# Product-key experts on one core: first gates written straight into their tile, one-hots made for four tokens at a time, first query group projected list by list

## The chip, the cores and the metric

One core of one Trainium2 chip runs the whole program. The metric is device time in microseconds (us) of one execution. Engines are named as in the profile: PE is TensorE (PEld its weight loads), DVE VectorE, ACT ScalarE, POOL GpSimd, SP SyncE, which issues most DMAs.

## The reference, cut to what matters

The program computes two transformer blocks over 512 tokens of width 1024. The change lies in the last part of the second block, a layer of 128 x 128 experts that are addressed by product keys:

```python
q = (t @ w_query).reshape(n_tok, P_HEADS, 2, P_DQ)            # 8 heads, 2 halves, 128 wide
sc = jnp.einsum('thcd,hckd->thck', q, sub_keys)               # 16 lists of 128 scores per token
s1, i1 = lax.top_k(sc[:, :, 0], P_TOPK)                       # best 16 of each list
s2, i2 = lax.top_k(sc[:, :, 1], P_TOPK)
cand = (s1[..., :, None] + s2[..., None, :]).reshape(n_tok, P_HEADS, P_TOPK * P_TOPK)
top_s, top_i = lax.top_k(cand, P_TOPK)                        # best 16 pairs of each head
e1 = jnp.take_along_axis(i1, top_i // P_TOPK, axis=-1)
e2 = jnp.take_along_axis(i2, top_i % P_TOPK, axis=-1)
gates = jax.nn.softmax(top_s, axis=-1)
act = jax.nn.gelu(einsum('td,tkd->tk', tb, expert_u[eb])) * gb
return einsum('tk,tkd->td', act, expert_v[eb])
```

## The kernel before, in words

Everything below is in `peer` and its helpers. The 512 tokens are four blocks of 128. Three blocks are "dense": for them all 16384 experts are computed, in 128 pieces of 128 experts, and a dense matrix of gates, zero where an expert was not chosen, weights them. The fourth block is "sparse": its chosen rows are gathered by indirect DMA.

**Queries and lists.** `w_query` is 1024 x 2048, that is 16 lists (head and half) of 128 columns. `proj` handles a group of four lists: for each of 8 row tiles of the weights it loads 128x512, ACT casts the high part (w_hi, L291), POOL subtracts to get the low part (w_lo, L293), and PE does three matmuls for each of four column blocks, so a list of the group is finished only when all four are, after 96 matmuls (L308, `acc`). `pick` then multiplies each block's queries with the keys (L2026, `sc`), ACT copies the scores (`scs`, L2029), and DVE takes the best 16 of each list (`top16`: five instructions, L2313 to L2317). `peer_pairs` forms candidate pairs on POOL (`cand`, `pr_w`, `pr_st`, `p_oh`) and picks the best 16 pairs on DVE. Its steps are mixed with the next lists.

**First pieces.** Each of the 128 pieces has a first half: load 128x1024 of `expert_u` (`p_raw`), cast (`p_hi`, ACT), subtract (`p_lo`, L2218, POOL for the first 13 pieces, then DVE), 24 matmuls into `pu`, gelu. 36 first halves (LAG) run ahead of the second halves; 15 (LEAD) are issued before the gates begin.

**Gates.** `peer_gates` (L2221 on) builds the gate matrix of the 384 dense tokens. For each token there are two one-hots of 128x128: o1 marks the first index, o2 the second, scaled by the gate; their product on PE (`pg`, L2235) is the 128x128 gates of that token. Before, each one-hot is a `tensor_scalar` with the index (and gate) as per-partition scalars: o2 always on DVE (L2234), o1 on DVE or POOL (L2232), eight buffers each. Four tokens fill one PSUM tile; ACT copies it into `gst` (L2236). Every 16 tokens ACT's queue writes 1 MB to the DRAM tensor `gates_d`. There are 96 such groups of four tokens, mixed with first halves of pieces 15 on.

**Second halves.** `load_gates` (L2071) reads 8 pieces' gates (`gt`, 1.5 MB) from `gates_d` on SP's queue. DVE multiplies `act` with them (L2082), ACT and DVE split the product (`ahi`, `alo`), and PE accumulates `py`. From there PE alternates between `pu` of piece c and `py` of piece c - 36.

The order of each engine's instructions is fixed when the program is built, by a scheduler that hoists instructions of the written order; each engine then runs its own list in order and waits where it must.

Of the kernel before, what the change touches and what calls it, by code (L numbers as in the profile page):

```python
# [9 lines left out]
F32 = mybir.dt.float32  # L10
# [3 lines left out]
U32 = mybir.dt.uint32  # L14
AF = mybir.ActivationFunctionType
ALU = mybir.AluOpType
# [4 lines left out]
P = 128  # L21
D = 1024
S = 512
NB = S // P
# [154 lines left out]
class Net:  # L179
# [1023 lines left out]

        return self.mod_c[:, split * 8:split * 8 + 8, s]

    def proj2(self, c0, n, acts, evac, lo_eng=None):


        nc = self.nc
        w_ap = self.a["w_in_2"][0]  # L1210
        lo_eng = lo_eng or nc.vector
        nt = (n + P - 1) // P
        kt = min(KC, 512 // n)
        main, ctx = acts
        ps = [self.psa.tile([P, 512], F32, tag="acc", name="acc2") for _ in range(nt)]
        pc = self.psa.tile([P, 2, 256], F32, tag="acc", name="acc_c") if ctx is not None else None
        for kk in range(KC // kt):
            raw = self.ws.tile([P, 512], F32, tag="w_raw", name="w_raw", bufs=3)[:, :kt * n].rearrange("p (k c) -> p k c", k=kt)
            nc.sync.dma_start(out=raw, in_=w_ap[kk * kt * P:(kk + 1) * kt * P, c0:c0 + n].rearrange("(k p) c -> p k c", p=P))
            hi = self.ws.tile([P, 512], F32R, tag="w_hi", name="w_hi")[:, :kt * n].rearrange("p (k c) -> p k c", k=kt)  # L1220
            lo = self.ws.tile([P, 512], F32R, tag="w_lo", name="w_lo")[:, :kt * n].rearrange("p (k c) -> p k c", k=kt)
            nc.scalar.copy(hi, raw)  # L1222
            lo_eng.tensor_tensor(lo, raw, hi.bitcast(F32), op=ALU.subtract)  # L1223
            for k2 in range(kt):
                k = kk * kt + k2
                st, sp = k == 0, k == KC - 1
                for j in range(nt):
                    m = min(P, n - j * P)
                    js = slice(j * P, j * P + m)
                    w = (hi[:, k2, js], lo[:, k2, js])  # L1230
                    self.mm3(ps[j][:m], w, main[k], st, sp)
                    if ctx is not None:
                        self.mm3(pc[:m, j], w, ctx[k], st and j == 0, sp, shared=True)
        for j in range(nt):
            evac(j, ps[j], pc[:, j] if ctx is not None else None)
# [739 lines left out]
    def peer(self):  # L1975
# [3 lines left out]
        nc, a = self.nc, self.a  # L1979
        tt, ts, stt = nc.vector.tensor_tensor, nc.vector.tensor_scalar, nc.vector.scalar_tensor_tensor  # L1980
        dense, sparse = range(ND), range(ND, NB)
        order = [*sparse, *dense]
        T = ND * P
# [7 lines left out]
        with self.pool("px") as xp:  # L1991
# [12 lines left out]
            hT = self.hT2  # L2004
# [12 lines left out]
        with self.pool("pe", 2, side="right") as ep:  # L2017
            best = {b: [tp.tile([P, 8, 16], F32, name=f"{n}{b}", bufs=1) for n in ("top", "e0", "e1")] for b in range(NB)}
            keys = tp.tile([P, 16, P], F32, name="pkeys", bufs=1)
            nc.sync.dma_start(out=keys, in_=a["sub_keys_2"].rearrange("h c d k -> d (h c) k"))  # L2020

            def pick(g, qT):
                for b in order:
                    ps = self.pt("sc").rearrange("p (n k) -> p n k", n=4)
                    for n in range(4):
                        nc.tensor.matmul(ps[:, n, :], qT[n][:, b * P:(b + 1) * P], keys[:, g * 4 + n, :],  # L2026
                                         start=True, stop=True)
                    sc = tp.tile([P, 4, P], F32, tag="sc", name="scs")
                    nc.scalar.copy(sc, ps)  # L2029
                    v16 = tp.tile([P, 4, 16], F32, tag="v16", name="v16", bufs=3)  # L2030
                    i16 = tp.tile([P, 4, 16], U32, tag="i16", name="i16", bufs=3)
                    i16f = tp.tile([P, 4, 16], F32, tag="i16f", name="i16f", bufs=3)
                    for n in range(4):
                        self.top16(v16[:, n, :], i16[:, n, :], sc[:, n, :], tp)
                        pending[:] = [p for p in pending if next(p, True) is None]
                        yield
                    nc.vector.tensor_copy(i16f, i16)
                    pending.append(pairs(g, b, v16, i16f))
# [4 lines left out]
                    self.peer_choice(best[b], tp, idx.get(b), gate.get(b), eg.get(b))  # L2043
            steps, pending = iter(()), []
            self.pool_turns = (0, 1, 2, 3)
            for g in range(4):
                qT = []

                def ev(j, ps):
                    t = tp.tile([P, S], F32, tag=f"pq{j}", name=f"pq{j}")  # L2050
                    nc.scalar.copy(t, ps)
                    qT.append(t)
                self.proj(a["w_query_2"][0], g * 512, hT, True, ev, between=lambda: [next(steps, None) for _ in range(2)])
                for _ in steps:
                    pass
                steps = pick(g, qT)
            dots = {b: ep.tile([P, P], F32, name=f"dots{b}", bufs=1) for b in sparse}
            y = {b: ep.tile([P, D], F32, name=f"py{b}", bufs=1) for b in sparse}
            acts, ps, gt = [], {}, []

            def first(c):
                hi, lo = self.peer_piece(a["expert_u_2_T"][c], ep, nc.gpsimd if c < LEAD - 2 else nc.vector)
# [6 lines left out]
                acts.append(act)  # L2069

            def load_gates(c):  # L2071
                t = sp.tile([P, T // 16, 8, 16], F32, tag="gt", name="gt")
                nc.sync.dma_start(out=t, in_=G[:, :, c:c + 8, :].rearrange("g p e t -> p g e t"))
                gt.append(t)

# [45 lines left out]
            n = 16  # L2121
            for c in range(LAG):
                if c == LEAD:
                    for _ in itertools.chain(steps, (x for p in pending for x in p)):
                        pass
                    tst.close()
                    gst = ExitStack()
                    gp = gst.enter_context(self.pool("pgs", 2))
                    steps = (None for b in dense for _ in self.peer_gates(b, eg[b], iota, G, gp))
                    n = T // 4  # L2130
                left = max((LEAD if c < LEAD else LAG - 3) - c, 1)
                first(c)
                for _ in range(-(-n // left)):
                    next(steps, None)
                    n -= 1
# [14 lines left out]
                nc.scalar.activation(out=junk, in_=o[:, hf * 512:(hf + 1) * 512], func=AF.Square, accum_out=ss[:, hf, b:b + 1])  # L2150

            with self.pool("ps", 2) as sp, self.pool("pu", 1, side="right") as gu:
                load_gates(0)
                held = []
                ps.update({(b, hf): self.psa.tile([P, 512], F32, tag="acc", name="py") for b in dense for hf in range(2)})
                for c in range(LAG, P + LAG):
                    if c < P:
                        first(c)
                    held.append(second(c - LAG))
                    ins = held[-1][1]  # L2160
                    if c < P + LAG - 2:
                        products(*held.pop()[0])
                    with self.tc.issue_after(ins.ins):
                        while done < 2 * P * len(sparse) and done * spread < c + 1 - LAG + min(c + 1, P) - LAG:
                            next(rows)
                            done += 1
                for b in sparse:
                    o = y[b]
                    nc.sync.dma_start(out=hN[b], in_=xd[b * P:(b + 1) * P, :])
                    tt(o, o, g2, op=ALU.mult)  # L2170
                    nc.gpsimd.tensor_tensor(o, o, hN[b], op=ALU.add)
                    for hf in range(2):
                        finish_squares(o, hf, b)

                for part in ((dense[:-1],), (dense[-1:], (0,)), (dense[-1:], (1,))):
                    for (args, _) in held:
                        products(*args, *part)
            with self.pool("pf") as fp:
# [18 lines left out]
                for b in (*sparse, *reversed(dense)):  # L2197
# [2 lines left out]
                    stt(o[:, 512:], o[:, 512:], rb, fw[:, 512:], op0=ALU.mult, op1=ALU.mult)  # L2200
                    nc.sync.dma_start(out=dst[b * 16:(b + 1) * 16], in_=o)
            fst.close()
            self.php_st.close()

    def gather(self, rows, idx, gu):
# [12 lines left out]
        (eng or self.nc.vector).tensor_tensor(lo, raw, hi.bitcast(F32), op=ALU.subtract)  # L2218
        return hi, lo

    def peer_gates(self, b, eg, iota, G, ep):  # L2221


        nc = self.nc
        for t in range(0, P, 4):
            if t % 16 == 0:
                st = ep.tile([P, P, 16], F32, tag="gst", name="gst")
            pg = self.tr("pg").rearrange("p (t e) -> p t e", t=4)
            for q in range(4):
                e1, e2, g = (eg[:, n, t + q:t + q + 1] for n in range(3))  # L2230
                o1 = ep.tile([P, P], F32, tag="oh1", name="oh1", bufs=8)
                (nc.vector if q >= 2 + t // 4 % 2 else nc.gpsimd).tensor_scalar(o1, iota, e1, None, op0=ALU.is_equal)  # L2232
                o2 = ep.tile([P, P], F32, tag="oh2", name="oh2", bufs=8)
                nc.vector.tensor_scalar(o2, iota, e2, g, op0=ALU.is_equal, op1=ALU.mult)  # L2234
                nc.tensor.matmul(pg[:, q, :], o2, o1, start=True, stop=True)  # L2235
            nc.scalar.copy(st.rearrange("p e t -> p t e")[:, t % 16:t % 16 + 4, :], pg)  # L2236
            if t % 16 == 12:
                nc.scalar.dma_start(out=G[(b * P + t) // 16], in_=st)
            yield

    def peer_pairs(self, v16, i16f, best, tp):
# [152 lines left out]
```

## Time and profile before

| What | Value |
| --- | --- |
| Median of 3 runs | 4377.47 us (4374.94 to 4378.69) |
| The profiled execution, its time | 4381.8 us |
| Its span | 4379.9 us, 59166 instructions |
| Busy share of the span | PE 93%, DVE 63%, ACT 38%, POOL 26% |
| Granted TensorE clock, mean | 0.965 |
| Queries begin on PE | 3003 us from the span's start |
| First `sc` product | 3033.80 us |
| One-hots begin on DVE | 3227.14 us |
| Last `pg` product done, `pu` alone follows | 3404.65 us |
| First `py` | 3424.66 us |

Times inside the execution are counted from the start of the span. The span ends 1.9 us short of the execution's time. A busy share averages over the whole program; the rows further down are cut to the stretch from 3003 us to 3520 us, where the change lies.

### The profile page before, as it was taken

How to read it: one execution, taken by the hardware profiler on the slowest of the kernel's cores; microseconds unless marked ns; L12 is line 12 of the kernel's file. 1: busy time of each engine (PE TensorE's matmuls, PEld its weight loads, DVE VectorE, ACT ScalarE, POOL GpSimd, SP SyncE). 2: the span in 40 equal slices, each digit the busy share in tenths (PEclk: the TensorE clock that was granted, in tenths of full speed). 3: DMA queues.
4: the chain of work that ended last, by engine and by line, in shares of the span. 5: the costliest groups of instructions: out<-in, count | busy, mean ns of one | idle time of the engine just before them, and what ended most of it. 6: DMA issues, size and time to landing. Idle time of an engine off the chain costs nothing. (4 is left out here: it accounts for less than half of the span.)

```text
span 4379.9 us, 59166 instructions
## 1 busy us (share of the span) xinstructions
PE 4054.2 (93%) x21308; PEld 3139.6 (72%) x21309; DVE 2778.6 (63%) x6214; ACT 1683.9 (38%) x3192; POOL 1150.9 (26%) x1089
## 2 busy tenths in 40 slices
PE   8999899999988998898898898898889899999998
PEld 6677544666665446777786777676679789988886
DVE  5455455553644556777767655636999777777776
ACT  4544211544441134445544444323256333333333
POOL 2001100100021013222102212125679344444443
PEclk9999999999999998989899999899999999999999
DMA  4145697222458951222121112134145988888875
GB/s 135 31 119 151 256 418 323 80 87 76 113 190 336 420 219 48 54 57 54 48 61 50 50 49 56 58 113 130 58 152 198 310 303 298 305 292 305 289 267 196
DMA packets 342588, 739.73 MB, mean 169 GB/s; under 512 B 72512, under 2 KB 175024, under 8 KB 314640
## 3 DMA queue, kind: packets, MB, share of 16 engines
q1 hardware_dynamic: 277536, 540.54, 36.9%
q0 software_dynamic: 45376, 167.76, 10.4%
q10 hardware_dynamic: 19376, 27.57, 1.7%
q8 instruction: 171, 2.80, 0.3%
q14 instruction: 129, 1.06, 0.1%
HBM read 694.07 MB, written 41.70 MB: 168 GB/s over the span
## 5 line engine op out<-in xcount | busy, mean ns | idle before, releaser
L308 PE MATMUL acc<-rn_hi,w_lo 128*128 128x512 f32 x1224 | 506.1, 414 | 36.9 <-DVE w_lo L1223 13.1
L308 PE MATMUL acc<-rn_hi,w_hi 128*128 128x512 f32 x1224 | 506.9, 415 | 32.3 <-ACT w_hi L1222 16.9
L308 PE MATMUL acc<-rn_lo,w_hi 128*128 128x512 f32 x1224 | 500.7, 409 | 2.0 <-POOL rn_lo L275 2.0
L293 POOL TENSOR_TENSOR w_lo<-w_raw,w_hi 128x512 fp32r<-128x512 f32 x103 | 136.3, 1325 | 1041.1 <-ACT w_hi L291 839.8
L2217 ACT CAST p_hi<-p_raw 128x1024 fp32r<-128x1024 f32 x256 | 268.4, 1049 | 333.5 <-PE pu L308 241.7
L308 PE MATMUL pu<-rn_hi,p_lo 128*128 128x384 f32 x1024 | 350.8, 343 | 17.7 <-POOL p_lo L2218 14.9
L291 ACT CAST w_hi<-w_raw 128x512 fp32r<-128x512 f32 x316 | 195.8, 621 | 435.0 <-PE acc L308 325.3
L308 PE MATMUL pu<-rn_hi,p_hi 128*128 128x384 f32 x1024 | 348.8, 341 | 5.3 <-ACT p_hi L2217 4.2
L308 PE MATMUL pu<-rn_lo,p_hi 128*128 128x384 f32 x1024 | 348.5, 340 | 0.0
L2218 DVE TENSOR_TENSOR p_lo<-p_raw,p_hi 128x1024 fp32r<-128x1024 f32 x243 | 297.4, 1224 | 73.2 <-ACT p_hi L2217 73.2
L293 DVE TENSOR_TENSOR w_lo<-w_raw,w_hi 128x512 fp32r<-128x512 f32 x213 | 149.7, 703 | 268.6 <-ACT w_hi L291 257.2
L308 PE MATMUL py<-p_hi,ahi 128*128 128x512 f32 x768 | 305.5, 398 | 6.6 <-ACT ahi L274 5.2
L308 PEld LDWEIGHTS acc<-rn_hi,w_lo 128*128 128x128 f32 x1224 | 237.5, 194 | 102.6 <-POOL w_lo L293 19.2
L308 PE MATMUL py<-p_lo,ahi 128*128 128x512 f32 x768 | 305.0, 397 | 2.3 <-DVE p_lo L2218 2.3
L308 PE MATMUL py<-p_hi,alo 128*128 128x512 f32 x768 | 304.9, 397 | 0.0
L308 PEld LDWEIGHTS acc<-rn_hi,w_hi 128*128 128x128 f32 x1224 | 237.4, 194 | 75.9 <-ACT w_hi L1222 19.3
L308 PEld LDWEIGHTS acc<-rn_lo,w_hi 128*128 128x128 f32 x1224 | 237.9, 194 | 34.8 <-POOL rn_lo L275 3.2
L2207 POOL DMA_INDIRECT eu<-in_expert_v_dram,idx x128 | 189.1, 1478 | 267.2 <-DVE py L2111 250.8
L2207 POOL DMA_INDIRECT eu<-in_expert_u_dram,idx x128 | 178.1, 1392 | 283.5 <-DVE dots L2097 271.8
L963 PE MATMUL gu<-wgu,xe 128*64 128x512 f32 x1024 | 242.6, 598 | 0.0
L308 PEld LDWEIGHTS pu<-rn_hi,p_lo 128*128 128x128 f32 x1024 | 194.7, 190 | 23.6 <-POOL p_lo L2218 18.1
L308 PEld LDWEIGHTS pu<-rn_hi,p_hi 128*128 128x128 f32 x1024 | 194.4, 190 | 11.6 <-ACT p_hi L2217 5.9
(736 smaller groups left out, 9528.9 us busy)
## 6 DMA issues: line engine op xcount, KB each, us to landing
w_raw<-in_w_in_dram SPq DMA_DIRECT2D x336, 256.0 KB, 2.7
p_raw<-in_expert_u_T_dram SPq DMA_DIRECT2D x128, 512.0 KB, 3.7
p_raw<-in_expert_v_dram SPq DMA_DIRECT2D x128, 512.0 KB, 4.9
wgu<-in_w_exp_gate_dram SPq DMA_DIRECT2D x62, 1024.0 KB, 12.2
wgu<-in_w_exp_up_dram SPq DMA_DIRECT2D x62, 1024.0 KB, 14.2
wdn<-in_w_exp_down_dram SPq DMA_DIRECT2D x60, 1024.0 KB, 12.8
ada_w<-in_w_ada_dram SPq DMA_DIRECT2D x96, 256.0 KB, 3.1
gates_d<-gst ACTq DMA_DIRECT2D x24, 1024.0 KB, 4.2
```

The costliest lines, as they stand in the source:

```text
L291: self.nc.scalar.copy(hi, raw)
L293: eng.tensor_tensor(lo, raw, hi.bitcast(F32), op=ALU.subtract)
L308: self.nc.tensor.matmul(ps, l, r, start=st, stop=sp or shared, skip_group_check=shared)
L963: nc.tensor.matmul(gu[64 * e:64 * e + 64, :], xe[:, c, 64 * e:64 * e + 64], wgu[e][:, :, c, :], start=c == 0, stop=c == KC - 1)
L2207: self.nc.gpsimd.indirect_dma_start(out=t, out_offset=None, in_=rows, in_offset=bass.IndirectOffsetOnAxis(ap=idx, axis=0))
L2217: self.nc.scalar.copy(hi, raw)
L2218: (eng or self.nc.vector).tensor_tensor(lo, raw, hi.bitcast(F32), op=ALU.subtract)
```

## The change

1. The first group of four lists no longer goes through `proj`. Each of its lists is projected by itself with `proj2` (weight tiles of 4 x 128 rows and 128 columns, low part on POOL), and a new `pick_first` scores one list for all four blocks. The pairs of the first group are put in one chain, block after block, when its fourth list is done. Groups 1 to 3 go as before.
2. `peer_gates` makes both one-hots of four tokens in one instruction each: two `tensor_tensor` compares on DVE of a broadcast `iota` with broadcast indices (128x4x128), then one `tensor_tensor` multiply with the broadcast gates on POOL. Three buffers each in place of eight.
3. The first 8 pieces' gates are copied from `gst` straight into their SBUF tile, by one more DMA on ACT's queue for every 16 tokens (64 KB), and the first `load_gates` goes away.

```diff
-    def proj2(self, c0, n, acts, evac, lo_eng=None):
+    def proj2(self, c0, n, acts, evac, lo_eng=None, w_ap=None):
...
+            first_v = {b: tp.tile([P, 4, 16], F32, name=f"v16_{b}", bufs=1) for b in range(NB)}
+            first_i = {b: tp.tile([P, 4, 16], F32, name=f"i16f_{b}", bufs=1) for b in range(NB)}
+
+            def pick_first(n, qT):
+                ps = self.pt("sc").rearrange("p (b k) -> p b k", b=NB)
+                for b in order:
+                    nc.tensor.matmul(ps[:, b, :], qT[:, b * P:(b + 1) * P], keys[:, n, :], start=True, stop=True)
+                sc = tp.tile([P, 4, P], F32, tag="sc", name="scs")
+                nc.scalar.copy(sc, ps)
+                i16 = tp.tile([P, 4, 16], U32, tag="i16", name="i16", bufs=3)
+                for b in order:
+                    self.top16(first_v[b][:, n, :], i16[:, b, :], sc[:, b, :], tp)
+                    nc.vector.tensor_copy(first_i[b][:, n, :], i16[:, b, :])
+                    yield
+                if n == 3:
+                    pending.append(itertools.chain(*(pairs(0, b, first_v[b], first_i[b]) for b in order)))
...
-            for g in range(4):
+            for n in range(4):
+                qT = tp.tile([P, S], F32, tag=f"pq{n}", name=f"pq{n}")
+                self.proj2(n * P, P, (hT, None), lambda _, ps, pc: nc.scalar.copy(qT, ps), nc.gpsimd, a["w_query_2"][0])
+                for _ in steps:
+                    pass
+                steps = pick_first(n, qT)
+            for g in range(1, 4):
...
-                t = sp.tile([P, T // 16, 8, 16], F32, tag="gt", name="gt")
+                t = gtp.tile([P, T // 16, 8, 16], F32, tag="gt", name="gt")
...
+                    gtp = gtst.enter_context(self.pool("pgt", 2))
+                    gt.append(gtp.tile([P, T // 16, 8, 16], F32, tag="gt", name="gt"))
...
-                load_gates(0)
...
+        sh = [P, 4, P]
+        iota4 = iota.unsqueeze(1).to_broadcast(sh)
...
+            e1, e2, g = (eg[:, n, t:t + 4].unsqueeze(2).to_broadcast(sh) for n in range(3))
+            o1, o2 = (ep.tile(sh, F32, tag=f"oh{n}", name=f"oh{n}", bufs=3) for n in (1, 2))
+            nc.vector.tensor_tensor(o1, iota4, e1, op=ALU.is_equal)
+            nc.vector.tensor_tensor(o2, iota4, e2, op=ALU.is_equal)
+            nc.gpsimd.tensor_tensor(o2, o2, g, op=ALU.mult)
             for q in range(4):
-                e1, e2, g = (eg[:, n, t + q:t + q + 1] for n in range(3))
-                o1 = ep.tile([P, P], F32, tag="oh1", name="oh1", bufs=8)
-                (nc.vector if q >= 2 + t // 4 % 2 else nc.gpsimd).tensor_scalar(o1, iota, e1, None, op0=ALU.is_equal)
-                o2 = ep.tile([P, P], F32, tag="oh2", name="oh2", bufs=8)
-                nc.vector.tensor_scalar(o2, iota, e2, g, op0=ALU.is_equal, op1=ALU.mult)
-                nc.tensor.matmul(pg[:, q, :], o2, o1, start=True, stop=True)
+                nc.tensor.matmul(pg[:, q, :], o2[:, q, :], o1[:, q, :], start=True, stop=True)
             nc.scalar.copy(st.rearrange("p e t -> p t e")[:, t % 16:t % 16 + 4, :], pg)
             if t % 16 == 12:
-                nc.scalar.dma_start(out=G[(b * P + t) // 16], in_=st)
+                n = (b * P + t) // 16
+                nc.scalar.dma_start(out=g0[:, n], in_=st[:, 0:8, :])
+                nc.scalar.dma_start(out=G[n], in_=st)
```

PE, where the first scores stand (`sc` is a score tile, `pq` the queries, `acc` the queries' sums). Before, 108 query matmuls stand ahead of these four products, and each of the next groups of four stands 24 matmuls further:

```order
L308 MATMUL acc<-rn_lo,w_hi 128x512
L308 MATMUL acc<-rn_hi,w_lo 128x512
L2026 MATMUL sc<-pkeys,pq_25474 128x128
L2026 MATMUL sc<-pkeys,pq_25476 128x128
L2026 MATMUL sc<-pkeys,pq_25478 128x128
L2026 MATMUL sc<-pkeys,pq_25480 128x128
L308 MATMUL acc<-rn_hi,w_hi 128x512
```

Now:

```order
L308 MATMUL acc_25374<-rn_hi,w_hi 128x512
L308 MATMUL acc_25374<-rn_lo,w_hi 128x512
L308 MATMUL acc_25374<-rn_hi,w_lo 128x512
L2029 MATMUL sc<-pkeys,pq_25334 128x128 x4
L308 MATMUL acc_25449<-rn_hi,w_hi 128x512
```

The first products moved from 108 matmuls to 48 behind the start; the next three groups of the first lists follow after 24, 24 and 12 matmuls more, and then 96 matmuls stand ahead of the first scores of group 1 (204 in all, as before).

POOL, between the queries' low parts (`w_lo`) and the first pairs (`i16f` is the list indices that DVE casts). Before:

```order
L293 TENSOR_TENSOR w_lo<-w_raw,w_hi 128x512 x6
L2251 TENSOR_TENSOR cand<-v_25511 128x2x24
L2251 TENSOR_TENSOR cand<-v_25511 128x2x16
L2251 TENSOR_TENSOR cand<-v_25511 128x2x8
L2251 TENSOR_TENSOR cand<-v_25511 128x2x16
L2256 TENSOR_TENSOR pr_w<-i16f,pr_25288 128x2x16
```

Now:

```order
L1223 TENSOR_TENSOR w_lo<-w_raw,w_hi 128x512 x2
L293 TENSOR_TENSOR w_lo<-w_raw,w_hi 128x512 x2
L2286 TENSOR_TENSOR pr_w<-i16f_25333,pr_25288 128x2x16
L2288 TENSOR_TENSOR pr_st<-pr_w 128x32
L293 TENSOR_TENSOR w_lo<-w_raw,w_hi 128x512
```

The third low part of group 1 now stands behind a `pr_w` that needs DVE's cast of the fourth list's first block.

DVE, where the one-hots begin (`eg` holds indices and gates). Before:

```order
L2218 TENSOR_TENSOR p_lo<-p_raw,p_hi 128x1024
L2234 TENSOR_SCALAR oh_27716<-iota_p,eg_25276 128x128
L2234 TENSOR_SCALAR oh_27721<-iota_p,eg_25276 128x128
L2232 TENSOR_SCALAR oh_27724<-iota_p,eg_25276 128x128
L2234 TENSOR_SCALAR oh_27726<-iota_p,eg_25276 128x128
```

Now:

```order
L2244 TENSOR_TENSOR p_lo<-p_raw,p_hi 128x1024
L2259 TENSOR_TENSOR oh_27730<-iota_p,eg_25276 128x512
L2260 TENSOR_TENSOR oh_27731<-iota_p,eg_25276 128x512
L2259 TENSOR_TENSOR oh_27741<-iota_p,eg_25276 128x512
L2260 TENSOR_TENSOR oh_27742<-iota_p,eg_25276 128x512
```

528 one-hots of 128x128 on DVE became 192 of 128x512; POOL's 240 one-hots became 96 multiplies of 128x512, one behind each L2260. In both orders 16 `p_lo` of 128x1024 stand between DVE's first and last one-hot. PE has 399 `pu` matmuls ahead of its first `pg` before and 421 now, and 79 and 77 behind its last.

## Rows read from the trace of the kernel before

**Rows 1.** Busy time of each engine by stretch: us, PE, PEld, DVE, ACT, POOL, clock, DMA.

```profile
3003.00:3034.00 31.00, 28.55 (x110) 22.20 (x111) 1.66 (x3) 10.47 (x17) 18.48 (x12) 0.87 0.57 171
3034.00:3227.00 193.00, 159.72 (x809) 138.26 (x808) 186.06 (x967) 62.35 (x96) 125.32 (x164) 0.97 0.22 69
3227.00:3405.00 178.00, 170.94 (x1184) 160.63 (x1184) 160.57 (x546) 117.93 (x131) 163.67 (x242) 1.00 0.55 201
3405.00:3425.00 20.00, 14.23 (x80) 13.60 (x79) 5.87 (x8) 6.17 (x10) 1.18 (x2) 0.97 0.90 250
3425.00:3520.00 95.00, 86.43 (x389) 73.57 (x389) 78.29 (x127) 27.57 (x39) 32.57 (x26) 0.93 1.01 337
```

**Rows 2.** The chain of waits, 3200 to 3460 us: start, us, what.

```profile
3236.80 10.27 POOL oh L2232 x15
...
3406.00 8.04 DMA gates_d<-gst
3414.25 9.24 DMA gt<-gates_d
3424.66 7.01 PE py L308 x17
```

**Rows 3.** Timeline of PE in the query stage: start, us, instruction.

```profile
3010.95 0.39 PE L308 MATMUL acc<-rn_lo,w_hi 128*128 128x512 f32 x1
...
3033.80 1.05 PE L2026 MATMUL sc<-pkeys,pq 128*128 128x128 f32 x8
...
3060.67 1.05 PE L2026 MATMUL sc<-pkeys,pq 128*128 128x128 f32 x8
```

**Rows 4.** Timeline of DVE: its first list, its fifth, its first one-hots.

```profile
3035.50 0.49 DVE L2313 MAX8 v<-scs 128x8 f32<-128x128 f32 x2 [30.16 <-ACT scs L2029]
...
3040.50 0.23 DVE L2313 MAX8 top<-cand 128x8 f32<-128x64 f32 x1
...
3227.14 1.07 DVE L2234 TENSOR_SCALAR oh<-iota_p,eg 128x128 f32<-128x128 f32 x2
```

**Rows 5.** Groups by shape, 3227 to 3405 us: busy us, mean ns, idle before.

```profile
L2234 DVE TENSOR_SCALAR oh<-iota_p,eg 128x128 f32<-128x128 f32 x384 | 123.4, 367 | 15.0 <-PE pg L2235 14.7
L2232 DVE TENSOR_SCALAR oh<-iota_p,eg 128x128 f32<-128x128 f32 x144 | 44.0, 307 | 0.0
L2218 DVE TENSOR_TENSOR p_lo<-p_raw,p_hi 128x1024 fp32r<-128x1024 f32 x18 | 22.7, 1259 | 0.0
L2232 POOL TENSOR_SCALAR oh<-iota_p,eg 128x128 f32<-128x128 f32 x238 | 159.3, 688 | 11.8 <-PE pg L2235 11.6
L2235 PE MATMUL pg<-oh,oh 128*128 128x128 f32 x768 | 104.6, 282 | 7.1 <-POOL oh L2232 4.6 <-issue 0.8 <-DVE oh L2234 0.3
```

**Rows 6.** Groups by shape, 3034 to 3227 us: 128x512 broadcast operations.

```profile
L2267 DVE TENSOR_TENSOR p_oh<-plf,pr_start 128x512 f32<-128x512 f32 x16 | 11.3, 706 | 0.0
L2281 DVE TENSOR_TENSOR p_oh<-plf,iota_p 128x512 f32<-128x512 f32 x16 | 10.7, 670 | 0.0
L2282 POOL TENSOR_TENSOR p_oh<-p_oh,i16f 128x512 f32<-128x512 f32 x16 | 20.6, 1290 | 31.5 <-DVE p_oh L2281 30.0 <-PE acc L308 1.5
```

**Rows 7.** Timeline of DVE and POOL, 2886 to 2890 us: two-tensor operations on both.

```profile
2886.20 1.12 DVE L275 TENSOR_TENSOR m2l<-mgate,m2h 128x512 fp32r<-128x512 f32 x1 [0.87 <-ACT m2h L274]
...
2887.85 1.16 DVE L275 TENSOR_TENSOR m2l<-mgate,m2h 128x512 fp32r<-128x512 f32 x1
...
2886.73 1.73 POOL L1912 TENSOR_TENSOR mgate<-mgate,mgate 128x512 f32<-128x512 f32 x1
...
2888.42 1.73 POOL L1912 TENSOR_TENSOR mgate<-mgate,mgate 128x512 f32<-128x512 f32 x1
```

**Rows 8.** `cand` on POOL (min/median/max ns), and one of it beside DVE's L2267.

```profile
L2251 POOL TENSOR_TENSOR cand<-v x64: 211/244/1194, 3039.4 to 3211.9; 128x32 f32<-128x32 f32 x32, 128x48 f32<-128x48 f32 x16, 128x16 f32<-128x16 f32 x16
...
3068.12 0.72 DVE L2267 TENSOR_TENSOR p_oh<-plf,pr_start 128x512 f32<-128x512 f32 x1
...
3068.25 0.69 POOL L2251 TENSOR_TENSOR cand<-v 128x32 f32<-128x32 f32 x1
```

**Rows 9.** SP's DMA issues: the first two gate loads, 3405 us on.

```profile
3414.25 5.47 SPq L2073 DMA_DIRECT2D gt<-gates_d  x2
```

More of the change, by code (lines that the diff above doesn't have):

```diff
@@ L1204, in col @@
         return self.mod_c[:, split * 8:split * 8 + 8, s]
-    def proj2(self, c0, n, acts, evac, lo_eng=None):
+    def proj2(self, c0, n, acts, evac, lo_eng=None, w_ap=None):
         nc = self.nc
-        w_ap = self.a["w_in_2"][0]
+        w_ap = self.a["w_in_2"][0] if w_ap is None else w_ap
         lo_eng = lo_eng or nc.vector
@@ L2058, in peer @@
             y = {b: ep.tile([P, D], F32, name=f"py{b}", bufs=1) for b in sparse}
-            acts, ps, gt = [], {}, []
+            acts, ps, gt, gtst = [], {}, [], ExitStack()
             def first(c):
@@ L2126, in peer @@
                     tst.close()
+                    gtp = gtst.enter_context(self.pool("pgt", 2))
+                    gt.append(gtp.tile([P, T // 16, 8, 16], F32, tag="gt", name="gt"))
                     gst = ExitStack()
                     gp = gst.enter_context(self.pool("pgs", 2))
-                    steps = (None for b in dense for _ in self.peer_gates(b, eg[b], iota, G, gp))
+                    steps = (None for b in dense for _ in self.peer_gates(b, eg[b], iota, G, gt[0], gp))
                     n = T // 4
@@ L2202, in peer @@
             fst.close()
+            gtst.close()
             self.php_st.close()
@@ L2219, in peer_piece, with peer_gates @@
         return hi, lo
-    def peer_gates(self, b, eg, iota, G, ep):
+    def peer_gates(self, b, eg, iota, G, g0, ep):
         nc = self.nc
+        sh = [P, 4, P]
+        iota4 = iota.unsqueeze(1).to_broadcast(sh)
         for t in range(0, P, 4):
```

## Prediction

> **What bounds the kernel now.** I read the busy time by stretch first. From 3034 to 3227 us, the list stage, DVE is busy 186.06 of 193 us and PE 159.72: the lists on DVE set the pace, and PE waits here and there [rows 1]. From 3227 to 3405 us, the gate stage, PE is busy 170.94, POOL 163.67 and DVE 160.57 of 178 us: three engines are near full. The chain of waits says which of them decides: it runs through stretches of POOL's one-hots, 10.27 us at a time [rows 2], with PE's own work between them. From 3405 to 3425 us PE is busy 14.23 of 20 us: the last gates are written to DRAM (8.04 us) and read back (9.24 us), and the `pu` matmuls that PE has left do not cover that [rows 1, 2]. From 3425 to 3520 us the DMA share is 1.01: transfers are the bound there, and PE loses 95 - 86.4 = 8.6 us. After that PE is full until the end, so time won or lost before 3520 us goes to the end one for one.
>
> The sum is made against the profiled execution, 4381.8 us, which is 4.3 us over the median 4377.47; I take the difference over to the median.
>
> **Part 1, first lists one by one.** The first score products move from 108 query matmuls behind the start to 48. The 93 matmuls from 3010.95 to 3033.80 us take 0.246 us each [rows 3], so 60 fewer are 14.7 us: products at 3019.1 instead of 3033.8, and the first list on DVE 1.7 us behind them as now [rows 3, 4], at 3020.8. Four lists take 5.0 us (3035.50 to 3040.50) [rows 4], so 16 take 20, and as the fourth group's scores come only at about 3037 (108 matmuls and three groups of products), DVE is done with the group at about 3044. But then it has nothing: the next list needs all of group 1, and its scores stand behind 204 matmuls, as before, where they came at 3060.67 [rows 3]. PE has no spare there, and POOL's third low part of group 1 now stands behind `pr_w`, which waits for a DVE cast; I put 2 us on that (between 0 and 5). So DVE goes on at 3060.7 + 2 + 1.7 = 3064.4, after 20 us of idling. Before, it had worked nearly without a break since 3035.5, 28.9 us less some 2 of stalls; now it has 20 us of lists, about 3 of small casts and pairs behind it. It is 4 us behind instead of 14.7 ahead, and the rest of the work is the same. **One-hots begin 4 us later**, at 3231 (ends: 8 us earlier, if the pairs fill part of the hole; 10 us later).
>
> The sixteen small casts in place of four larger ones fall before that hole and are hidden by it. The weight tiles of the first group are the same 8 loads of 256 KB on SP in smaller pieces; five of them stand far ahead of their use, I cost them at nothing, and if they came late, the hole would cover up to 20 us.
>
> **Part 2, one-hots of four tokens.** Counted by engine, this looks like a gain. DVE has 123.4 + 44.0 us of one-hots now [rows 5] and would have 192 of 0.67 = 129 us by the row of the same kind of compare with broadcast operands [rows 6]; POOL goes from 159.3 [rows 5] to 96 of 1.29 = 124 us [rows 6]. If the engines ran beside each other, PE would be the bound.
>
> They don't run beside each other. Where DVE and POOL both have operations with two SBUF tensors of 128x512, each takes turns: DVE's take 1.12 and 1.16 us in place of 0.67, POOL's 1.73 in place of 1.29, and DVE's ends (2887.32, 2889.01) and POOL's (2888.46, 2890.15) are 1.69 us apart [rows 7]. That is the one plus the other with only the start-ups overlapped. Broadcast operands make no difference: beside L2267, which has the operands of the new compares, a POOL addition of 32 elements takes 0.69 us where the median is 0.244, and ends 0.10 us behind DVE's end [rows 8].
>
> So a group of four tokens costs one alternation, 1.69 us, and a second compare, 0.60 (0.67 with the start-up overlapped): 2.29 us. 96 groups are 220 us. The 16 `p_lo` among them are of the same kind, 1.26 us each [rows 5], 18 us with start-ups overlapped. With 2 us for the first group: 240 us, against 3404.65 - 3227.14 = 177.5 now (the last `pg` ends where the `pu` alone begin). **The gate stage becomes 62.5 us longer.** PE's work there (at most 171 us) and ACT's (118 us and 24 more DMA issues) fit inside. Three buffers allow DVE two groups' lead over POOL, enough, since it is the sum of both that counts. The bounds of a group are 2.2 us (every start-up hidden) and 2.63 us (none, two of 0.67 and 1.29); I take the value near the rows in which both engines were queued up, [rows 7].
>
> The Trainium skill, page "SBUF — State Buffer", section "Who interferes with whom", speaks against the change in the same sense: a DVE instruction with two SBUF inputs contends with a GpSimd one that reads SBUF, and the second to issue is blocked until the first has finished. Taken as whole instructions, it would give 2.63 us a group and a stage of 272 us; the rows show 1.69 where whole instructions would be 1.96, and I go by the rows.
>
> **Part 3, first gates straight.** The read of `gt` (9.24 us in the chain [rows 2]) leaves the path. The 64 KB copies are issued ahead of the 1 MB write that now takes 8.04 us; behind the last `pg` stand 77 `pu`, some 13.5 us by the 79 that fill most of 14.23 us [rows 1], which cover a copy and DVE's and ACT's work on `act`. PE's idle 5.8 us of that stretch go: **5.8 us less**. Two loads are issued together on SP now, 5.47 us [rows 9]; one remains, still behind the last write, with the `p_raw` loads queued behind it. As PE also starts `py` sooner after the last `pg`, I cost the stretch limited by DMA at no change (4 us either way).
>
> **Sum**: 4 + 62.5 - 5.8 = 60.7 us. 4381.8 becomes 4442.5, the median 4377.5 becomes **4438 us**.
>
> **Rivals.**
>
> A. *No turns in this pair of operations* (a multiply in place, a compare whose second operand has step zero). Then PE's 170.9 us are the bound, less the 22 `pu` that move ahead of the stage, about 167 us: 10 us less, and with 4 - 5.8 a total of -12: 4366, faster. For it: POOL and DVE are both busy over 160 of 178 us now. Against it: the rows on L2267. It decides if a group falls under 1.85 us. Chance 0.06.
>
> B. *The lists keep their lead.* If the scheduler's order lets DVE work in the hole, one-hots begin up to 14.7 us earlier instead of 4 later: 4420. For it: in the stage as a whole DVE is the bound. Against it: group 1's scores cannot come before its 204th matmul. Chance 0.13.
>
> C. *Turns at full price*, 2.63 us a group: 96 x 2.63 + 20 = 272 us, 32 more: 4471. For it: each hand-over needs a signal between engines, which the alternation of [rows 7], already queued, does not show. Chance 0.12.
>
> D. *The first gates are still late*: the copies queue behind 1 MB writes, and the 5.8 us stay: 4444. This lies within the forecast's own range.
>
> **How the numbers follow.** The forecast with D has 0.69 and its own range is 4420 to 4460: 2.2 to 2.45 us a group (-9 to +15), lists from -12 to +6 about the value taken, the load up to +6; these are not all at their ends together. B adds to the low side and C to the high side. The range 4408 to 4468 leaves out A, the top of C and the tails. 0.2% is 8.8 us, about what a measurement of this kernel can tell from no change. Slower: the forecast, B and C, 0.93; faster: most of A, 0.04; the same 0.03, where A is weak or the terms cancel.
>
> **What would show it.** In the profile after: the first list on DVE near 3021 us, then an idle of 15 to 20 us ended by the scores of group 1; one-hots from about 3231 to 3470 us; in that stretch DVE and POOL with records longer than 0.67 and 1.29 us that end in turn, PE idle for a third, waiting for POOL's `oh`; no wait for `ahi` at the first `py`. I am wrong in the main step if the 96 multiplies stay at 1.29 us beside compares of 0.67 us and the stage is under 180 us.

## The result, and the profile after

| | median us | runs | lowest to highest |
|---|---|---|---|
| before | 4376.99 | 4 | 4374.94 to 4378.69 |
| changed | 4430.35 | 4 | 4428.14 to 4433.32 |

The ratio is 1.0126, 95% interval 1.0110 to 1.0142: **53.4 us slower**. The forecast was 60.7 us slower, 4438. The profiled execution of the changed kernel took 4433.32 us with a span of 4431.6, 51.7 more than the span before.

First the busy time by stretch of the changed kernel, with the columns of [rows 1] (the last two numbers of a row are the DMA share and GB/s); the bounds are moved to where its stages lie.

```profile
3003.00:3235.00 232.00, 194.76 (x932) 170.08 (x932) 192.72 (x981) 76.49 (x115) 138.82 (x173) 0.92 0.25 80
3235.00:3457.00 222.00, 175.86 (x1172) 160.84 (x1171) 211.93 (x210) 116.81 (x130) 137.53 (x98) 0.98 0.43 160
3457.00:3479.00 22.00, 15.45 (x78) 14.81 (x77) 10.37 (x17) 6.12 (x9) 3.95 (x5) 0.84 0.93 309
3479.00:3574.00 95.00, 89.15 (x430) 77.72 (x429) 78.64 (x125) 30.48 (x42) 38.29 (x29) 0.98 1.03 347
```

The gate stage is now 222 us long instead of 178, and DVE fills it (211.93), while PE has about the same work as in [rows 1] (1172 matmuls, 1184 there) and idles 46 us. DVE's own work did not grow by count: 210 instructions stand where 546 stood. The groups by shape of that stretch, as in [rows 5], show what filled it.

```profile
L2261 POOL TENSOR_TENSOR oh<-oh,eg 128x512 f32<-128x512 f32 x96 | 136.5, 1422 | 84.4 <-DVE oh L2260 65.6 <-PE pg L2263 18.1 <-PE pu L308 0.7
L2260 DVE TENSOR_TENSOR oh<-iota_p,eg 128x512 f32<-128x512 f32 x96 | 124.3, 1295 | 0.0
L2263 PE MATMUL pg<-oh,oh 128*128 128x128 f32 x768 | 106.5, 286 | 40.3 <-POOL oh L2261 39.2 <-ACT gst L2264 0.3
...
L2259 DVE TENSOR_TENSOR oh<-iota_p,eg 128x512 f32<-128x512 f32 x96 | 81.9, 853 | 6.5 <-PE pg L2263 6.5
```

The two compares are the same operation on the same shape; one takes 0.85 us in the mean and the other 1.30, without an idle time ahead of it. PE waits 39.2 us for POOL's product. The timelines of DVE and POOL show how one group goes.

```profile
3283.18 0.68 DVE L2259 TENSOR_TENSOR oh<-iota_p,eg 128x512 f32<-128x512 f32 x1
3283.79 1.52 DVE L2260 TENSOR_TENSOR oh<-iota_p,eg 128x512 f32<-128x512 f32 x1
3285.23 0.68 DVE L2259 TENSOR_TENSOR oh<-iota_p,eg 128x512 f32<-128x512 f32 x1
3285.83 1.52 DVE L2260 TENSOR_TENSOR oh<-iota_p,eg 128x512 f32<-128x512 f32 x1
...
3283.40 1.36 POOL L2261 TENSOR_TENSOR oh<-oh,eg 128x512 f32<-128x512 f32 x1 [1.29 <-PE pg L2263]
3285.45 1.36 POOL L2261 TENSOR_TENSOR oh<-oh,eg 128x512 f32<-128x512 f32 x1 [0.69 <-DVE oh L2260]
```

The compare that has POOL's multiply beside it takes 1.52, the other 0.68, and a group takes 3285.83 - 3283.79 = 2.04 us.

For the lists, PE's products and DVE's idle times, the counterpart of [rows 3, 4]:

```profile
3018.52 1.05 PE L2029 MATMUL sc<-pkeys,pq 128*128 128x128 f32 x8
...
3034.98 1.05 PE L2029 MATMUL sc<-pkeys,pq 128*128 128x128 f32 x8
...
3059.14 1.06 PE L2044 MATMUL sc<-pkeys,pq 128*128 128x128 f32 x8
...
3021.29 0.49 DVE L2343 MAX8 v<-scs 128x8 f32<-128x128 f32 x2 [16.17 <-ACT scs L2031]
...
3060.85 0.49 DVE L2343 MAX8 v<-scs 128x8 f32<-128x128 f32 x2 [13.20 <-ACT scs L2047]
...
3235.26 0.68 DVE L2259 TENSOR_TENSOR oh<-iota_p,eg 128x512 f32<-128x512 f32 x1
```

The first list comes at 3021.29, as forecast. The fourth group's products come at 3034.98, those of group 1 only at 3059.14, and DVE idles 13.2 us between them (the hole, below). One-hots begin 8.1 us later than in [rows 4].

Behind the gates, DVE's timeline and the waits of PE:

```profile
3452.23 1.21 DVE L2244 TENSOR_TENSOR p_lo<-p_raw,p_hi 128x1024 fp32r<-128x1024 f32 x1
3464.83 3.37 DVE L2106 TENSOR_TENSOR act<-act,gt 128x384 f32<-128x384 f32 x7 [11.39 <-issue]
3468.12 2.35 DVE L2244 TENSOR_TENSOR p_lo<-p_raw,p_hi 128x1024 fp32r<-128x1024 f32 x2
...
3463.39 0.44 PE L308 MATMUL pu<-rn_hi,p_hi 128*128 128x384 f32 x1 [1.16 <-ACT p_hi L2243]
...
3469.39 0.69 PE L308 MATMUL pu<-rn_hi,p_lo 128*128 128x384 f32 x1 [5.39 <-DVE p_lo L2244]
```

PE no longer waits for `ahi` at its first `py`. It waits 5.39 us for a `p_lo` that stands in DVE's order behind seven products `act` x gates. For the 11.39 us that DVE waits ahead of these, this profile names no releaser; the last copy into the tile was issued at 3457.94. In the run with the first gates alone, further down, the profile names the copy for the same wait:

```profile
3412.56 3.37 DVE L2082 TENSOR_TENSOR act<-act,gt 128x384 f32<-128x384 f32 x7 [8.22 <-DMA gt<-gst]
```

To add this up I measure each stage from rows of the same kind: the first `acc` matmul of the queries, the first one-hot, the start of the last copy `gst`, the first `py`.

| kernel (profiled run) | queries to one-hots | one-hots to last `gst` | `gst` to first `py` |
|---|---|---|---|
| before | 223.7 | 177.8 | 19.8 |
| changed | 232.0 | 221.6 | 22.1 |
| lists alone | 232.4 | 176.9 | 18.9 |
| one-hots alone | 223.0 | 223.2 | 17.9 |
| first gates alone | 223.4 | 181.1 | 18.2 |
| changed, one-hots as before | 232.6 | 181.5 | 19.2 |

The three differences, from the unrounded times, are 8.3 + 43.8 + 2.4 = 54.5; the rest up to the end is 2.6 shorter and the queries begin 0.2 earlier: 51.7 us, the difference of the spans.

### The profile page after: what moved, and what is told of

Read it like the earlier page. It is cut to its first block, busy times and chain, and to the rows that moved or that the text cites. A ratio compares the mean times of both kernels' runs of the same rounds, so it can differ in the third digit from the quotient of the medians.

```text
span 4431.6 us, 58766 instructions
## 1 busy us (share of the span) xinstructions
PE 4055.9 (92%) x21308; PEld 3141.9 (71%) x21309; DVE 2837.3 (64%) x5890; ACT 1685.7 (38%) x3194; POOL 1124.0 (25%) x945
## 5 line engine op out<-in xcount | busy, mean ns | idle before, releaser
L293 POOL TENSOR_TENSOR w_lo<-w_raw,w_hi 128x512 fp32r<-128x512 f32 x95 | 126.1, 1329 | 1036.1 <-ACT w_hi L291 821.9
```

## Experiments: the three parts, one at a time

Three kernels are the kernel before with one part of the diff each; the fourth is the changed kernel with the old one-hots. The theory is the forecast's: DVE and POOL take turns. Every ratio is against the kernel before in the same set of runs, whose median was 4379.67 us in this set, 4385.52 for the multiply on DVE, the four buffers, the multiply token by token and the late `p_lo` on POOL, and 4381.23 for the POOL multiplies that nobody reads and the lists of two and four groups.

**The changed kernel without the new one-hots**

```
-            nc.vector.tensor_tensor(o1, iota4, e1, op=ALU.is_equal)
-            nc.vector.tensor_tensor(o2, iota4, e2, op=ALU.is_equal)
-            nc.gpsimd.tensor_tensor(o2, o2, g, op=ALU.mult)
...
+                (nc.vector if q >= 2 + t // 4 % 2 else nc.gpsimd).tensor_scalar(o1, iota, e1, None, op0=ALU.is_equal)
...
+                nc.vector.tensor_scalar(o2, iota, e2, g, op0=ALU.is_equal, op1=ALU.mult)
```

> The changed kernel with the one-hots token by token as before; the lists list by list and the first gates straight stay. Turn-taking (the cost lies in DVE and POOL taking turns in the gate stage): the stage falls from 221 us to about 177.5, and only the lists' 8 us and 1 or 2 us of the first gates stay, so 4385 (4380 to 4390), 44 under the changed kernel. Rival 'lists' (the later start of the one-hots makes what follows late, and the stage is long since POOL's and DVE's other work falls into it): the time stays over 4415. If the stretch behind the gates gained what I forecast, 4379.

Measured 4390.22, ratio 1.0022 (1.0012 to 1.0032). Some 43 us of the 53 went with the one-hots; the time lies at the upper end of what was expected.

**The new one-hots alone**: the lines with a minus above, put into the kernel before.

> The kernel before with the new one-hots alone. Turn-taking: the gate stage takes 221 us instead of 177.5 and starts at the same 3227 us, so 4377 + 44 = 4421 (4414 to 4428). Rival 'lists': under 4390. Rival 'sum is not of parts' (the stage is long only together with the first gates' copies on ACT's queue): 4395 to 4410.

Measured 4418.59, ratio 1.0087 (1.0072 to 1.0101): 38.9 us. The row of the copies `gst` gives the end of the stage in this run. One-hots begin 223.0 us behind the queries (223.7 in the kernel before), and the stage lasts 223.2 us, 45 longer.

```profile
L2238 ACT COPY gst<-pg x96: 1017/1058/1114, 3227.0 to 3445.2; 128x512 f32<-128x512 f32 x96
```

**The lists alone**: `proj2`, `pick_first` and the loop over the first four lists.

> The kernel before with the first lists list by list alone. By the trace after, one-hots start 8 us later (3235.3 instead of 3227.1), so 4385 (4381 to 4389). Rival: the later start there is caused by the p_lo that DVE takes ahead of the one-hots and is made up in the gate stage, which then is shorter: 4377 to 4379, within 0.1%.

Measured 4389.63, ratio 1.0021 (1.0012 to 1.0029): 10.0 us. Its one-hots begin 232.4 us behind the queries, as in the changed kernel, and the gate stage does not make it up (176.9 against 177.8).

**The first gates alone**: the tile `g0`, the copies into it, no first load.

> The kernel before with the first gates straight from their tile alone. My forecast's term: 5.8 us less, 4371. By the trace after, where PE waited for DVE's p_lo behind seven products act x gates that wait for the last copy: the wait only changes its name, 4377 (4374 to 4380), and DVE's first product still waits some 10 us.

Measured 4383.05, ratio 1.0009 (0.9998 to 1.0019): no gain, and no loss that can be told from none; the expected 4374 to 4380 was missed by 3 us. The three parts alone cost 38.9 + 10.0 + 3.4 = 52.3 us, the whole change 53.4: they add up within the noise.

## Experiments: what makes the gate stage long

**The multiply on DVE**

```
-            nc.gpsimd.tensor_tensor(o2, o2, g, op=ALU.mult)
+            nc.vector.tensor_tensor(o2, o2, g, op=ALU.mult)
```

> The changed kernel with the gate multiply issued on DVE instead of POOL; POOL has no one-hot work left. Turn-taking: DVE has three operations of 0.60 us a group back to back (0.67 with the start-up overlapped), 96 x 1.8 = 173, and 17 p_lo of 1.22, 21: a stage of about 194 instead of 221 us, so 4430 - 27 = 4403 (4398 to 4412), faster although DVE does all the work alone. Rival 'side by side' (the two engines do overlap, and the stage is long for the signals and the three buffers): DVE's work grows by 96 x 0.6 = 58 us and the time does not fall: 4430 or more.

Measured 4406.36, ratio 1.0043 (1.0027 to 1.0058) against 1.0126: 20.8 us over the kernel before instead of 53.4, with all the one-hot work on one engine. The stage is 193.0 us (expected 194). This takes a hand-over (a tile passed on from one engine to another by a signal) out as well as the turns, so it does not yet tell the two apart.

**Four buffers**: `bufs=3` becomes `bufs=4` in the changed kernel.

> The changed kernel with four buffers for each of the two one-hot tiles instead of three. Turn-taking: the sum of both engines' holds does not change, 4430 (4426 to 4434), and the group's period stays 2.05 us. Rival 'buffers' (DVE waits for PE to give an old tile back, POOL for DVE): a fourth of the 44 us or more goes, 4419 or less.

Measured 4432.96, ratio 1.0103 (1.0087 to 1.0118); the intervals of this kernel and the changed one overlap. DVE's wait for PE to give a tile back falls from 6.5 to 1.7 us, and the stage is 219.7 us instead of 221.6. The buffers are at most a small part of what holds it.

**The multiply token by token**, two on POOL and two on ACT:

```
-            nc.gpsimd.tensor_tensor(o2, o2, g, op=ALU.mult)
+            for q in range(4):
+                gq = eg[:, 2, t + q:t + q + 1]
+                if q < 2:
+                    nc.gpsimd.tensor_scalar(o2[:, q, :], o2[:, q, :], gq, None, op0=ALU.mult)
+                else:
+                    nc.scalar.activation(out=o2[:, q, :], in_=o2[:, q, :], func=AF.Copy, scale=gq)
```

> The changed kernel with the gate multiply token by token, in a form with one SBUF tensor and a scalar per partition: two tokens of each group on POOL, two on ACT. DVE's compares stay. Turn-taking: the compares fall to 0.67 us each (mean now 0.85 and 1.30), POOL has 192 multiplies of about 0.66 (its compares of that shape before), 127 us, ACT 118 + 192 x 0.3 = 176: the stage falls to between 175 and 190 us, so 4385 to 4400. Rival 'side by side with hand-over cost': the hand-overs from DVE to another engine and on to PE stay, and there are more of them: the stage stays over 215 us, 4425 or more, with compares over 0.85.

Measured 4462.77, ratio 1.0183 (1.0168 to 1.0199): a miss in time, where the rival 'side by side with hand-over cost' had wanted 4425 or more, and a hit in the records. The compares did fall to 0.69 us, where that rival had wanted over 0.85, but the stage grew to 249.7 us. The groups by shape show why:

```profile
L2268 PE MATMUL pg<-oh,oh 128*128 128x128 f32 x766 | 132.9, 317 | 48.2 <-ACT gst L2269 23.2 <-POOL oh L2264 18.3 <-ACT oh L2266 5.0
...
L2259 DVE TENSOR_TENSOR oh<-iota_p,eg 128x512 f32<-128x512 f32 x93 | 65.0, 699 | 95.2 <-PE pg L2268 95.0
```

DVE waits 95 us for PE to give back a tile, and PE waits 23.2 us for ACT's copies `gst` and 23.3 for the scaled one-hots. ACT now has both in one order, each product behind a copy that waits for PE. I read this as a ring of hand-overs, which was not tried by itself. If so, hand-overs alone can make this stage long, and the next pair was made to have none.

**POOL multiplies that nobody reads**, beside the kernel with the multiply on DVE, of two SBUF tensors or of one:

```
             nc.vector.tensor_tensor(o2, o2, g, op=ALU.mult)
+            jk = ep.tile(sh, F32, tag="jk", name="jk", bufs=1)
+            nc.gpsimd.tensor_tensor(jk, iota4, g, op=ALU.mult)                # two tensors
+            nc.gpsimd.tensor_scalar(jk, iota4, 2.0, None, op0=ALU.mult)       # or one
```

> The kernel with the multiply on DVE, and beside it one POOL multiply per group of two SBUF tensors of 128x512 into a tile that nobody reads (its values don't enter the output). No engine waits for it, so there is no hand-over in it. Turn-taking: 96 of DVE's operations alternate with 96 of POOL's at 1.69 us a pair, the other 192 take 0.60, and 17 p_lo 21: a stage of about 298 instead of 192 us, 4406 + 105 = 4510 (4480 to 4535), with DVE's compares well over 0.75 us. Rival 'hand-over' (what costs is the passing from DVE to POOL to PE): nobody waits for POOL, so 4406 (4400 to 4412) and compares as they are, 0.75.

> As the run with POOL multiplies of two tensors that nobody reads, but each has one SBUF tensor and a constant. Turn-taking needs two tensors on both sides: the time is that of the kernel with the multiply on DVE, 4406 (4400 to 4412), and DVE's operations keep their mean of 0.75 us. Rival 'any POOL work of this size holds DVE off': as the run with two tensors, over 4470.

Two tensors: 4487.57, ratio 1.0249 (1.0233 to 1.0264), 81 us over the kernel with the multiply on DVE (4406.36), or 85 when each is taken against the kernel before of its own set, inside the expected 4480 to 4535, where 'hand-over' wanted no difference. The stage is 273.2 us against 193.0, 80 longer. The timelines of POOL and DVE in that run:

```profile
3232.39 140.53 POOL L2263 TENSOR_TENSOR jk<-iota_p,eg 128x512 f32<-128x512 f32 x96
...
3288.98 1.37 POOL L2263 TENSOR_TENSOR jk<-iota_p,eg 128x512 f32<-128x512 f32 x1
3290.43 1.37 POOL L2263 TENSOR_TENSOR jk<-iota_p,eg 128x512 f32<-128x512 f32 x1
...
3289.37 1.52 DVE L2259 TENSOR_TENSOR oh<-iota_p,eg 128x512 f32<-128x512 f32 x1
3290.82 1.52 DVE L2261 TENSOR_TENSOR oh<-oh,eg 128x512 f32<-128x512 f32 x1
3292.26 1.52 DVE L2260 TENSOR_TENSOR oh<-iota_p,eg 128x512 f32<-128x512 f32 x1
```

As long as POOL's 96 operations last, 140.53 us, POOL and DVE both work with hardly a gap, and each operation on either begins 1.45 us behind the last: one of DVE's, one of POOL's, in strict turn. Without POOL they are 0.60 apart in the kernel with the multiply on DVE:

```profile
3289.80 0.72 DVE L2259 TENSOR_TENSOR oh<-iota_p,eg 128x512 f32<-128x512 f32 x1
3290.40 0.73 DVE L2261 TENSOR_TENSOR oh<-oh,eg 128x512 f32<-128x512 f32 x1
3291.00 0.73 DVE L2260 TENSOR_TENSOR oh<-iota_p,eg 128x512 f32<-128x512 f32 x1
```

1.45 + 0.60 = 2.05 us: the group of the changed kernel. A turn adds 1.45 - 0.60 = 0.85 us, and 96 of them 82, about what the stage grew by. No engine waits for POOL's result here, so the turns are shown, and the price of one.

One tensor: 4447.09, ratio 1.0152 (1.0138 to 1.0167), 41 us over (45 against the own sets), neither theory's number. The stage is 232.2 us, 39 longer. DVE's operations are alternately plain and 0.41 us longer, one for each of POOL's (96 x 0.41 = 39):

```profile
3228.85 159.48 POOL L2263 TENSOR_SCALAR jk<-iota_p 128x512 f32<-128x512 f32 x96
...
3289.33 0.68 DVE L2261 TENSOR_TENSOR oh<-oh,eg 128x512 f32<-128x512 f32 x1
3289.94 1.09 DVE L2260 TENSOR_TENSOR oh<-iota_p,eg 128x512 f32<-128x512 f32 x1
3290.95 0.68 DVE L2259 TENSOR_TENSOR oh<-iota_p,eg 128x512 f32<-128x512 f32 x1
```

So my "needs two tensors on both sides" falls: one tensor on POOL's side also holds DVE, for about half as long (0.41 against 0.85).

## Experiments: the lists and the first gates

**Lists of two groups, and of all four, list by list.** `pick_first` runs over 8 or 16 lists, its casts join four lists again, and the pairs of later groups stand in one line (two groups) or in two (four groups). The edit, cut, against the lists alone:

```
-            for n in range(4):
+            for n in range(8):
...
-                    nc.vector.tensor_copy(first_i[b][:, n, :], i16[:, b, :])
+                    if j == 3:
+                        nc.vector.tensor_copy(first_i[g, b], first_u[g, b])
```

> The kernel before with the lists of the first two groups (not of the first alone) made list by list, and their indices cast four lists at a time as before. If the lists' 8 us come from the hole of 13.2 us in which DVE waits for all four queries of group 1, and from the smaller casts: the hole closes, DVE goes from 3021 us on with the same work as before, and the one-hots begin 8 to 12 us earlier than before: 4368 to 4372. Rival 'DVE has no work to start earlier on' (the pairs of the first group stand behind one another and their steps wait for POOL at the end): one-hots no earlier, 4380 or more.

> As the run with two groups list by list, with all four. By the hole alone: no further gain, 4366 to 4374, since DVE is busy from group 1 on in either. Rival 'the last scores come late' (with one list of all blocks at a time the last pairs of all four blocks come together at the end, and their steps on DVE and POOL are in line behind each other): the one-hots begin later than with two groups, 4380 or more.

Measured 4386.48 (1.0012, 1.0003 to 1.0021) and 4386.74 (1.0014, 1.0003 to 1.0025), beside 4381.23. Both missed what was expected (4368 to 4372 and 4366 to 4374); the rivals' 4380 or more came. By the medians both recover about half of what the lists alone cost (1.0021), but the intervals overlap, and neither is faster than the kernel before. With two groups the hole moved on to group 2 (9.4 us). With four it is gone, the last list begins at 3184.1 us, 24 us nearer to the queries than before, and one-hots still begin 229.2 us behind the queries. Two groups by shape of that run say where that went:

```profile
L2302 DVE TENSOR_TENSOR p_oh<-plf,pr_start 128x512 f32<-128x512 f32 x16 | 21.2, 1327 | 0.0
...
L2320 DVE TENSOR_REDUCE e<-p_oh 128x32 f32<-128x512 f32 x16 | 10.8, 676 | 3.4 <-POOL p_oh L2317 3.1
```

The pairs' first compare takes 1.33 us in the mean where it took 0.71 [rows 6], 10 us in all; with POOL at two-tensor work beside it, turns are the likely reason, but that was not tried by itself. From 3200 to 3234 us DVE is busy 24.03 of 34 us: the pairs now come at the end, where each step waits for the last on POOL, PE or ACT. DVE's work had not only to begin earlier, it had to be at hand in the right order.

**First gates alone, with the late `p_lo` on POOL**

```
-            hi, lo = self.peer_piece(a["expert_u_2_T"][c], ep, nc.gpsimd if c < LEAD - 2 else nc.vector)
+            hi, lo = self.peer_piece(a["expert_u_2_T"][c], ep, nc.gpsimd if c < LEAD - 2 or LAG - 3 <= c < LAG + 2 else nc.vector)
```

> The kernel before with the first gates straight, and the p_lo of the first queries' pieces 33 to 37 on POOL instead of DVE, where two of them stood behind seven products act x gates that wait for the last copy (PE idled 6.7 us for that in the run with the first gates straight alone). If that order of DVE's ate the gain: PE's idle goes, and the time is 6 us under that run, 4377 (4373 to 4380). Rival 'the copy itself is late' (it lands some 8 us behind its issue, like the write it replaced): PE then waits for ahi in place of p_lo, 4381 to 4384, no better.

Measured 4393.35, ratio 1.0023 (1.0014 to 1.0032); the run without this edit had 1.0009. No gain, so the first theory's time was missed, and the rival's wait did not come either: PE's idle behind the gates did go, as the windows show (18 us behind the last `gst`, the 97 after them, and both), but it came back at once.

```profile
3409.00:3427.00 18.00, 17.50 (x92) 15.83 (x92) 8.77 (x12) 6.82 (x11) 10.79 (x8) 1.00 0.83 283
3427.00:3524.00 97.00, 81.58 (x378) 70.46 (x377) 76.89 (x123) 27.40 (x37) 37.05 (x28) 0.94 1.05 354
3409.00:3524.00 115.00, 99.08 (x468) 86.29 (x468) 85.66 (x135) 34.22 (x48) 47.84 (x36) 0.95 1.01 343
```

PE is busy 99.1 of those 115 us, against 14.23 + 86.43 = 100.7 in the kernel before [rows 1] and 101.7 with the first gates alone, at DMA shares of 1.01, 0.99 and 1.04. PE's first wait of 5.44 us comes 15 us later, for a `p_hi`, and SP spent 8.91 us on the issue of a load of `p_raw` ahead of it. I read transfers as the bound of the whole stretch; no run took any out. Two things in this run's trace keep it from settling what DVE's order costs. Two of the five `p_lo`, 2.4 us each, fell among POOL's one-hots, and the gate stage is 186.3 us against 181.1 with the first gates alone. And DVE's first product began 2.8 us behind the issue of the last copy, against 7.2 there, so a quicker copy can have taken the idle away as well. Why the gate stage is 3 to 5 us longer with the copies and the old one-hots (181.1 against 177.8, 181.5 against 176.9) was not tried.

No version of these beats the kernel before.

## Why the prediction was right in sign and 7 us too high

**Part 2, the main step, was right in mechanism and mis-sized in one term.** "A group of four tokens costs one alternation, 1.69 us, and a second compare, 0.60": the alternation is 1.45 in this pair. 96 x (1.45 + 0.60) = 197, and the 16 `p_lo` between the one-hots, 1.14 from start to start, are 18. These 215 us compare with 217.0 measured from the first one-hot to the `p_lo` behind the last, of which 6.5 are waits for PE; some compares escape the full turn, so that the means of 0.85 and 1.30, less their overlaps, make 2.00 a group. The last multiply, products and copy add 4.6. The forecast had 240 (+62.5) and got 221.6 (+43.8). The 1.69 came from another pair, a product of two whole tensors and a low part [rows 7]; the case itself lies below my lower bound of 2.2 a group. POOL's 1.42 us and DVE's 0.85 and 1.30 are the records that I named as its mark; PE idles 46 of 222 us, a fifth and not the third that I named. Rivals A (no turns) and C (2.63) are out. A's limit of 1.85 us a group is the old stage over 96 groups (177.5 / 96), without the `p_lo`; with their 18 us it is 1.66, and so the 1.80 us a group of DVE alone are still slower than the old form.

The Trainium skill, page "SBUF — State Buffer", section "Who interferes with whom", says that a DVE instruction with two SBUF inputs contends with a GpSimd one that reads SBUF. The run with two POOL tensors agrees in strict turns, at 1.45 us a pair. The run with one POOL tensor, which reads SBUF too, shows 0.41 us, not a full turn.

**Part 1 was right in the first list, the fourth group and the hole, and wrong in what is left behind it.** The forecast had DVE go on at 3064.4 and need 166.6 us more. It went on at 3060.85 and needed 174.4. The hole was 13.2 us and not 20, since the casts kept DVE busy till 3047.6 and group 1's scores came at 3059.14, 1.5 us before those of [rows 3] and not 2 behind: PE waited 1.0 us for the `w_lo` behind `pr_w`, and in the kernel before it waits 1.6 us for `w_lo` in the same stretch. "The rest of the work is the same" failed: of those 174.4 us DVE was busy 165.3 and idle 9.1, where the kernel before idles 3.8 us from the same point on (3062.4), and the forecast left about as much. In the whole stage DVE waited 7.5 us for the pairs' products on POOL (4.5 before), and the pairs' second compare took 0.93 us in the mean (0.67 in [rows 6]). Counted from the first list to the one-hots: 13.2 of hole, 3.8 more of other idling and 5.3 more of work (28 casts of 0.48 us in place of 16 of 0.50 make 5.4, the rest cancels) are 22.3; the first list came 14.0 earlier; 8.3 remain.

**Part 3 was wrong.** "5.8 us less" did not come: D, which I had inside the forecast's range, is what happened, in another form. The read left the path, but the first products still waited 6.9 us behind the issue of the last copy, and DVE's order put two `p_lo` behind them. PE's idle in the stretch is 6.6 us (22 - 15.45), 5.8 before. With the `p_lo` on POOL that idle went and PE's waits came in the stretch limited by DMA, which I had costed at "no change (4 us either way)". One thing stays open. From the last `gst` to the end of the span the first gates alone take 970.0 us against 975.0 before, and the changed kernel with the old one-hots 971.3 against 974.3 with the lists alone, with gate stages 3.3 and 4.6 us longer; the changed kernel takes 974.7 against 970.5 with the one-hots alone, with a gate stage 1.6 us shorter. That is one trace for each, and the runs of the first gates alone lie between 4376.71 and 4398.81, so whether a part of the gain came and was taken back by the gate stage is not shown.

Against the spans, the errors were -18.7 (gates), +4.3 (lists), +8.2 (behind the gates) and -2.8 (the rest up to the end and the start of the queries): 51.7 where 60.7 was forecast. Two steps that were too hopeful hid two thirds of one that was too dark, so that the total is off by only 7 is in part luck.

Rival B (lists keep their lead) failed for the reason given against it: group 1's scores came behind the 204th matmul.

## What to carry to other kernels

Before work is split between DVE and POOL, look for a place in the trace where both run that pair of operations at once, and price the pair, not each engine: here one engine alone (1.80 us a group) beat two in turn (2.05), and both lost to the old form, whose operations had one SBUF tensor and a scalar each. An earlier start is worth only what the next input allows: the 14 us of the first lists went into the wait for group 1 and into pairs that were not ready sooner. A wait taken out in front of a stretch that is full of transfers can come back inside it, as it did here.

## What the runs showed of the hardware

- The price of a turn depends on the pair of operations: 1.45 us for a compare or multiply with a broadcast operand on DVE beside such a multiply on POOL, 1.69 for the pair of [rows 7]. In both, DVE's operation ends some 0.55 us behind POOL's; POOL's ends 1.14 us behind DVE's in [rows 7] and 0.91 with the POOL multiplies that nobody reads (3291.80 and 3290.89), so POOL's part of the turn makes the difference. Which operand does it was not tried.
- A POOL operation of 128x512 with one SBUF tensor and a constant lengthens one DVE operation by 0.41 us. POOL's 128x128 products with a scalar per partition did not show it: the compares of that run had medians of 0.692 and 0.684 us. Those products themselves took 0.60 us in the median and up to 2.10; the cause was not tried.
